# Pieces of 384 tokens in the first third of a projection sweep

## The chip, the cores and the metric

The kernel runs on one core of a Trainium2 chip. The metric is the device time of one execution in microseconds (us). Profiles are of single executions, so their times stand a little off the median of the timed runs.

The engines are called as in the profile: PE is the matrix engine (PEld its weight loads, which overlap the products), DVE the vector engine, ACT the scalar engine, POOL GpSimd; SP only issues DMAs. An instruction queue runs in order.

## The reference

One step of a decoder layer for a prompt of 2048 tokens and a sample group of 8 x 4 = 32 tokens, with shared weights:

```
h   = RMSNorm(x) @ w_in        # D_MODEL 1024 -> 9472 columns
qa, ka, va, za, ub, zb, qc, zc, gt = split(h)
oa  = dilated sliding-window attention(qa, ka, va)   # 12 heads x 64, three (window, dilation) patterns
ob  = silu(LayerNorm(causal depthwise conv, width 31, of GLU(ub)))
oc  = cross-attention(qc) into 256 memory tokens      # 4 heads x 128
mix = gate0 * ((oa * silu(za)) @ w_pa) + gate1 * ((ob * silu(zb)) @ w_pb)
    + gate2 * ((oc * silu(zc)) @ w_pc)                # gates = sigmoid(gt)
y   = x + RMSNorm(mix @ w_out)
```

The sample group attends to caches of past keys and values. All data are float32.

## The kernel before

**Arithmetic.** A float32 product is made of three products of rounded operands: the activations x and the weights w are each split into a high and a low part, and `gemm` adds whi·xh (L166), whi·xl (L167) and wlo·xh (L168). The weights (128 x 128) are the stationary operand and the tokens the moving one, so a product has as many columns as the piece has tokens. With 8 blocks of 128 rows in D_MODEL, a piece of tokens of one block of 128 output columns takes 24 products into one PSUM tile.

**Stages.** `phase_a1` normalizes and transposes x, and computes the q, k, v, u and qc columns (PSUM tile `g`). Behind it come, in the order of the program text: `memory` (which holds the convolution branch's norm `conv_norm` on the tiles `c`, `sm`, `sq`, the memory's keys and values, and both cross-attentions), `sample_attention`, `attention` over 12 heads, then `sweep`, then `phase_c` (gates, projections and the output).

**The sweep.** `sweep` computes the remaining columns of `w_in`: 40 blocks, namely 6 of za, 6 of zb, 4 of zc and 24 of gt. SBUF holds the split activations of one third of the tokens only (tiles `x0h`, `x0l`, 16 in all). So the sweep runs through all 40 blocks for the first third, then refills the 16 tiles from DRAM (`d_x`, issued on POOL's queue at L1083), runs through all 40 blocks again for the second third, and so on. A block's weights are loaded (`wraw`, from ACT's queue) and split on POOL (L55 `whi`, L56 `wlo`) once per third, into two buffers. Within a third the inner loop runs over pieces:

```
SCHUNKS = [(256 * i, 256) for i in range(7)] + [(1792, 288)]     # (first token, tokens)
THIRDS = [(0, 768), (768, 768), (1536, 544)]
...
for s, m in SCHUNKS:
    if a <= s < a + n:
        self.chunk(kind, j, s, m, w, stg, ps, "gg", q=nc.scalar)
        yield
```

**A piece.** `chunk` takes one of two PSUM tiles `gg` (pool `pgg`), each of 512 columns, and one of two SBUF tiles `st` of 384 columns. The 24 products fill `gg`. A gt piece is then read out by one tanh on ACT (L243); a za, zb or zc piece by a tanh on ACT (L245) and a multiply on DVE (L246) that reads `gg` too. A store to DRAM (`d_g`, `d_za`, `d_zb`, `d_zc`) is issued on ACT's queue (L248).

**What sets the order.** The kernel is written with a framework that lays out each engine's order when the program is built. A position in the program text is a priority, and the framework's own estimates of durations say when an operand is ready. The sweep's text stands behind all of `attention`, so it has the lowest priority of the four and fills places in which the others have nothing ready. On the chip that order is fixed: an engine runs its queue in order and waits on semaphores.

Of the kernel before, what the change touches and what calls it, by code (L numbers as in the profile page):

```python
# [28 lines left out]

GROUPS = [(0, 3), (3, 6), (6, 9), (9, 12), (12, 14), (14, 17)]  # L30
CHUNKS = [(0, 384), (384, 384), (768, 384), (1152, 384), (1536, 256), (1792, 288)]
SCHUNKS = [(256 * i, 256) for i in range(7)] + [(1792, 288)]
THIRDS = [(0, 768), (768, 768), (1536, 544)]

CQ, CK, CV, CZA, CUB, CZB, CQC, CZC, CGT = 0, 768, 1536, 2304, 3072, 4608, 5376, 5888, 6400
# [2 lines left out]
class K:  # L38
# [1036 lines left out]
    def sweep(self, blocks, xp, wp, stg, ps):  # L1075
        nc = self.nc
        for th, (a, n) in enumerate(THIRDS):
# [8 lines left out]
            for kind, j in blocks:  # L1086
                w = self.early.pop((kind, j), None) if th == 0 else None
                w = w or self.load_w(wp, self.win(self.BASE[kind] + 128 * j), 8, q=nc.scalar, bufs=2, rp=stg)
                for s, m in SCHUNKS:
                    if a <= s < a + n:  # L1090
# [217 lines left out]
```

## Time and profile before

| | us |
|---|---|
| median of 3 runs | 3149.05 (3148.02 to 3153.83) |
| the profiled execution | 3154.4 |
| its span, from the first to the last instruction | 3152.6 |
| first product of the sweep starts | 868.7 |
| last product of the sweep starts | 2549.7 |
| refills of `x0` are issued | from 1432.1 and up to 2110.5 |

The mean clock that PE was granted is 0.979 of full speed. To read the views: "A <- B" in a list of waits says that A sat idle until B had finished. The chain that ended last is followed back from the last instruction, at each step to what released it or to the instruction before it on its engine; an engine's share of it says how much of the time that engine set. A product's busy time holds its latency and overlaps with its neighbours', so the pace of PE is read from the distance of starts.

### The profile page before, as it was taken

What the parts mean: (1) busy time and instruction counts of PE and PEld (TensorE: products, weight loads), DVE (VectorE), ACT (ScalarE), POOL (GpSimd) and SP (SyncE); (2) the same over time, 40 slices, a digit from 0 to 9 for tenths busy, and PEclk for the clock granted to TensorE, in tenths of its full rate; (3) what the DMA queues carried; (4) which work ended last, traced back from release to release, by engine and by line L of the source; (5) the groups of instructions that cost most, each with busy time, mean ns of one, the idle gap of its engine ahead of it and who ended that gap; (6) DMA issues with size and microseconds to landing.
All of it is one profiled execution on the core that took longest, in us unless ns stands there. A gap on an engine that the chain in (4) does not pass through costs nothing.

```text
span 3152.6 us, 55374 instructions
## 1 busy us (share of the span) xinstructions
PE 3000.2 (95%) x20705; PEld 2839.9 (90%) x20705; DVE 2014.8 (64%) x3734; ACT 1124.2 (36%) x2835; POOL 1350.4 (43%) x1048
## 2 busy tenths in 40 slices
PE   7999999999987999999999999989899979999998
PEld 6899999999987999998999999989898967787897
DVE  5297797796677926465546766666656457556563
ACT  5010010010132433243437575656565523222221
POOL 0121221142356537444256565667676433233240
PEclk9899999999999999999999999999999989999999
DMA  7232222211265454477454656576555487657561
GB/s 250 85 103 80 80 60 61 63 62 50 81 182 167 135 153 144 147 219 239 151 139 116 161 123 163 128 185 150 156 143 152 109 279 227 223 168 227 161 197 53
DMA packets 532218, 454.66 MB, mean 144 GB/s; under 512 B 118191, under 2 KB 458581, under 8 KB 531137
## 3 DMA queue, kind: packets, MB, share of 16 engines
q1 hardware_dynamic: 357502, 335.36, 36.2%
q10 hardware_dynamic: 169840, 105.02, 11.7%
q0 software_dynamic: 4608, 10.75, 1.2%
q8 instruction: 164, 2.69, 0.4%
q14 instruction: 104, 0.85, 0.1%
HBM read 332.96 MB, written 118.04 MB: 143 GB/s over the span
## 4 chain that ended last, share of the span: by engine, by line
PE 70%; DMA 12%; DVE 7%; issue 4%; POOL 3%; ACT 2%; SPq 1%; ACTq 0%; DVEq 0%; POOLq 0%
PE g L166 8%; PE g L167 8%; PE g L168 8%; PE gg L166 6%; PE gg L168 6%; PE gg L167 6%; PE pg L168 3%; PE pg L166 3%; PE pg L167 3%; PE pt L571 2%; DMA cb<-d_cf 2%; PE y L1180 2%; PE y L1179 2%; PE y L1178 2%; PE o L598 1%
## 5 line engine op out<-in xcount | busy, mean ns | idle before, releaser
L166 PE MATMUL gg<-x0h,whi 128*128 128x256 f32 (+1 forms) x2560 | 747.9, 292 | 25.9 <-DVE st L246 12.2
L168 PE MATMUL gg<-x0h,wlo 128*128 128x256 f32 (+1 forms) x2560 | 741.8, 290 | 0.1
L167 PE MATMUL gg<-x0l,whi 128*128 128x256 f32 (+1 forms) x2560 | 741.1, 290 | 0.0
L55 POOL TENSOR_SCALAR whi<-wraw 128x1024 fp32r<-128x1024 f32 x162 | 242.7, 1500 | 928.5 <-PE g L167 524.1
L166 PEld LDWEIGHTS gg<-x0h,whi 128*128 128x128 f32 x2560 | 493.2, 193 | 35.0 <-DVE st L246 13.7
L167 PEld LDWEIGHTS gg<-x0l,whi 128*128 128x128 f32 x2560 | 493.5, 193 | 2.2 <-issue 0.5
L168 PEld LDWEIGHTS gg<-x0h,wlo 128*128 128x128 f32 x2560 | 493.2, 193 | 2.2 <-POOL wlo L56 0.3
L322 DVE SCALAR_TENSOR_TENSOR acc<-G,cw,acc 128x1536 f32<-128x1536 f32 (+15 forms) x354 | 480.8, 1408 | 0.3
L56 POOL TENSOR_TENSOR wlo<-wraw,whi 128x1024 fp32r<-128x1024 f32 x162 | 417.0, 2575 | 9.4 <-PE gg L168 0.2
L155 POOL TENSOR_TENSOR clo<-craw,chi 128x768 fp32r<-128x768 f32 (+1 forms) x96 | 174.1, 1815 | 346.0 <-ACT chi L154 329.8
L627 ACT ACTIVATE P<-T,stm 128x128 f32<-128x128 f32 (+1 forms) x576 | 260.8, 455 | 141.0 <-DVE stm L625 94.8
L239 ACT ACTIVATE st<-g 128x384 f32<-128x384 f32 (+1 forms) x132 | 60.2, 461 | 570.7 <-PE g L168 550.7
L166 PE MATMUL pg<-ac,chi 128*128 128x512 f32 (+1 forms) x640 | 229.4, 359 | 16.6 <-ACT chi L154 8.7
L625 DVE CUSTOM_DVE_ANT_0 T<-s,bias 128x128 f32<-128x128 f32 (+1 forms) x576 | 191.5, 357 | 80.8 <-PE s L617 47.0
L167 PE MATMUL pg<-ac,chi 128*128 128x512 f32 (+1 forms) x640 | 228.8, 358 | 6.3 <-DVE ac L1198 6.3
L168 PE MATMUL pg<-ac,clo 128*128 128x512 f32 (+1 forms) x640 | 227.6, 357 | 3.6 <-POOL clo L155 3.6
L576 DVE TENSOR_TENSOR pl<-pt,ph 128x512 fp32r<-128x512 f32 x240 | 155.6, 652 | 52.4 <-ACT ph L575 48.9
L168 PE MATMUL g<-x0h,wlo 128*128 128x384 f32 x544 | 184.3, 339 | 2.9 <-POOL wlo L56 2.9
L166 PE MATMUL g<-x0h,whi 128*128 128x384 f32 x544 | 183.6, 338 | 2.6 <-ACT st L239 2.3
L167 PE MATMUL g<-x1l,whi 128*128 128x384 f32 x544 | 186.0, 342 | 0.0
L167 PE MATMUL g<-x0l,whi 128*128 128x384 f32 x544 | 185.8, 342 | 0.0
L168 PE MATMUL g<-x1h,wlo 128*128 128x384 f32 x544 | 185.8, 342 | 0.0
(330 smaller groups left out, 7425.0 us busy)
## 6 DMA issues: line engine op xcount, KB each, us to landing
wraw<-in_w_in ACTq DMA_DIRECT2D x119, 512.0 KB
d_g<-st ACTq DMA_DIRECT2D x168, 128.0 KB
cb<-d_cf SPq DMA_DIRECT2D x72, 256.0 KB
g<-d_g SPq DMA_DIRECT2D x72, 256.0 KB
wraw<-in_w_in SPq DMA_DIRECT2D x35, 512.0 KB
kvc<-in_cache_k_win SPq DMA_DIRECT2D x8, 1536.0 KB
kvc<-in_cache_v_win SPq DMA_DIRECT2D x8, 1536.0 KB
raw<-d_q SPq DMA_DIRECT2D x48, 256.0 KB
```

Source lines behind the costliest of these rows:

```text
L55: nc.gpsimd.tensor_scalar(hi, raw, 1.0, 1.0, op0=ALU.mult, op1=ALU.mult)
L56: nc.gpsimd.tensor_sub(lo, raw, hi.bitcast(F32))
L155: nc.gpsimd.tensor_sub(lo, raw, hi.bitcast(F32))
L166: nc.tensor.matmul(ps, hi[:, k, :], h, start=k == 0, stop=False)
L167: nc.tensor.matmul(ps, hi[:, k, :], l, start=False, stop=False)
L168: nc.tensor.matmul(ps, lo[:, k, :], h, start=False, stop=k == kb - 1)
L322: nc.vector.scalar_tensor_tensor(a3[:, lo:hi], G[:, src:src + hi - lo, 2 - m:130 - m], w, a3[:, lo:hi], op0=ALU.mult, op1=ALU.add)
L571: nc.tensor.transpose(t[:, 128 * x:128 * x + 128], pc, self.ident)
L576: nc.vector.tensor_tensor(pl[:, :w], t[:, :w], ph[:, :w].bitcast(F32), op=ALU.subtract)
L625: nc.vector.tensor_tensor_reduce(sc[:, :w], t[:, o:o + w], bias[:, 256 - w:256], 1.0, 3.0e38, ALU.add, ALU.min, m)
L627: nc.scalar.activation(P[:, o:o + w], sc[:, :w], AF.Exp, bias=m, scale=-1.0, accum_out=self.stl[:, col:col + 1])
L1178: nc.tensor.matmul(y[:m, c, :], ah[:, ts_], bh[:, cs], start=k == 0, stop=False)
```

## The change

The pieces of the first third become two of 384 tokens in place of three of 256. The second third keeps three pieces of 256, the last third its pieces of 256 and 288.

```diff
 CHUNKS = [(0, 384), (384, 384), (768, 384), (1152, 384), (1536, 256), (1792, 288)]
-SCHUNKS = [(256 * i, 256) for i in range(7)] + [(1792, 288)]
+SCHUNKS = [(0, 384), (384, 384)] + [(256 * i, 256) for i in range(3, 7)] + [(1792, 288)]
 THIRDS = [(0, 768), (768, 768), (1536, 544)]
```

No tile changes its size: `gg` has 512 columns and `st` has 384 in both.

## The prediction

> **What bounds the kernel now.** The page comes first: which engine fills the span, and which ends it.
>
> ```profile
> span 3152.6 us, 55374 instructions
> PE 3000.2 (95%) x20705; PEld 2839.9 (90%) x20705; DVE 2014.8 (64%) x3734; ACT 1124.2 (36%) x2835; POOL 1350.4 (43%) x1048
> PE 70%; DMA 12%; DVE 7%; issue 4%; POOL 3%; ACT 2%; SPq 1%; ACTq 0%; DVEq 0%; POOLq 0%
> ```
>
> PE is busy for 95% of the span and makes 70% of the chain that ended last; no other engine comes near. A faster PE therefore pays, but only where PE is what the chain follows. So the second view is the table by stretch, for the time in which the sweep's first third runs: the first row ends where DVE has finished its last piece of that third, the second about where the third ends. Of each stretch I show all work, then the tile `gg` (the sweep's products) alone. Columns: length, then busy time and count on PE, on PEld and on the others.
>
> ```profile
> 868.70:1118.00 249.30, 212.54 (x1638) 204.79 (x1637) 202.72 (x264) 91.54 (x171) 141.68 (x126) 0.95 0.53 162
> 1118.00:1435.00 317.00, 314.23 (x2502) 301.96 (x2502) 151.34 (x329) 114.27 (x286) 162.76 (x182) 1.00 0.54 168
> 868.70:1118.00 249.30, 163.89 (x1171) 152.15 (x1172) 19.36 (x48) 18.30 (x48) 0.95 0.53 162
> 1118.00:1435.00 317.00, 227.28 (x1700) 212.50 (x1700) 0.00 (x0) 27.20 (x71) 1.00 0.54 168
> ```
>
> The two stretches differ. In the first PE has 37 us idle and DVE is busy for 203 of 249; in the second PE is never idle for longer than 3 us in all. 1171 of the first third's 2880 products lie in the first stretch, 1700 in the second. The third view, the chain cut to those stretches and to what follows up to the end of the attention, says which engine sets the pace.
>
> ```profile
> by line: issue 16.1%; DVE c L685 9.7%; PE gg L166 6.2%; PE gg L167 5.8%; PE gg L168 5.7%; POOL c L681 4.7%; DVE sm L665 4.6%; DVE sm L673 3.7%; DMA wraw<-in_w_mem_kv 3.5%; ACT sq L684 2.9%; DMA c<-d_c 2.8%; DVE st L246 1.9%; ACT sq L671 1.8
> by line: PE gg L166 19.2%; PE gg L168 19.2%; PE gg L167 19.2%; PE co L990 4.5%; PE tr L791 4.4%; PE sco L1034 4.4%; PE S L804 3.8%; DMA kvc<-in_cache_k_win 3.6%; PE tr L862 2.9%; PE pt L981 2.8%; PE sco L1058 2.5%; PE str L1029 1.9%; PE kv
> by line: PE gg L166 10.5%; PE gg L168 10.2%; PE gg L167 10.1%; PE pt L571 6.4%; DMA cb<-d_cf 4.6%; PE o L598 4.4%; PE s L616 4.2%; PE s L617 4.2%; PE o L597 4.0%; issue 4.0%; DMA rv<-out_v_win_p 2.3%; DMA wraw<-in_w_in 2.1%; DMA x0h<-d_x 2.
> ```
>
> In the first stretch the chain is the convolution branch's norm (`c`, `sm`, `sq` on DVE, ACT and POOL), and `gg` has 17.7% of it. In the second `gg` alone has 57.6% and almost everything else is PE too. Behind it (third row) the chain is again mostly PE, with the attention's products: what the first third gives up earlier, the attention takes over earlier.
>
> **The change part by part.** *Fewer products.* A block of the first third takes 3 pieces of 24 products of 256 columns now, and 2 pieces of 24 of 384 then: 72 become 48, over 40 blocks 2880 become 1920, for the same columns. What that saves hangs on the part of a product's cost that doesn't grow with its columns. The busy times overlap and can't say; the distance of starts can. Each pair below is the first and the last of an unbroken run: 256 columns in the sweep (14 rows), then 384 on the same tile (11 rows) and on another (19 rows), and 256 in a slow moment of the sweep (11 rows), whose granted clock, 0.50, stands in the last row.
>
> ```profile
> 1203.13 0.28 PE L168 MATMUL gg<-x0h,wlo 128*128 128x256 f32 x1
> 1204.69 0.28 PE L166 MATMUL gg<-x0h,whi 128*128 128x256 f32 x1
> ...
> 299.83 0.33 PE L168 MATMUL g<-x0h,wlo 128*128 128x384 f32 x1
> 301.56 0.34 PE L166 MATMUL g<-x0h,whi 128*128 128x384 f32 x1
> ...
> 599.73 0.34 PE L166 MATMUL g<-x1h,whi 128*128 128x384 f32 x1
> 602.90 0.34 PE L166 MATMUL g<-x1h,whi 128*128 128x384 f32 x1
> ...
> 959.45 0.41 PE L167 MATMUL gg<-x0l,whi 128*128 128x256 f32 x1
> 961.58 0.41 PE L168 MATMUL gg<-x0h,wlo 128*128 128x256 f32 x1
> ```
>
> ```profile
> 959.00:961.60 2.60, 2.60 (x14) 2.51 (x13) 2.60 (x5) 2.03 (x3) 0.98 (x1) 0.50 0.96 314
> ```
>
> 1.56/13 is 120 ns for 256 columns; 1.73/10 is 173 ns and 3.17/18 is 176 ns for 384. Three old products cost 360 ns; two new ones 346 or 352. I take 348, nearest the row on the same tile: 12 ns saved per three, or 3.3%. There are 960 such threes, so PE gives up 11.5 us (bounds 7.7 and 13.4).
>
> The Trainium skill, "TensorE: Matmul & The Clock Gate", section "Back-to-back issue gap", speaks against this: at full clock a lone product's gap is its columns by 2.4 GHz and about 2.5 ns, so 109 and 162.5 ns here. By it the saving is some 2.5 ns per three, an estimate of 2.4 us in all. The trace disagrees: 120 and 173.
>
> What of the 11.5 us lies on the path? In the second stretch PE is the path: 1700/3 threes at 12 ns are 6.8 us, and by the chain 57.6% of 317 us at 3.3% is 6.0; I take **6.5**. In the first stretch only the chain's 17.7% of 249.3 us, 44 us, shrinks by 3.3%: **1.5**. The other 3 us of the first stretch become PE idle time in front of the norm's products.
>
> *Fewer, longer evictions.* `gg` has two PSUM buffers, so a piece starts when the piece before last has been read out. That is the one place in which PE waits for the sweep itself (waits of PE in 868 to 1120 us, then the longest of 1120 to 1445):
>
> ```profile
> PE sco L675 <- DVE sm L673: 14.9, 5, 9.0
> PE gg L166 <- DVE st L246: 10.1, 9, 1.8
> ...
> PE S L804 <- ACT KTh L794: 2.8, 1, 2.8
> ```
>
> ```profile
> L243 ACT ACTIVATE st<-gg 128x256 f32<-128x256 f32 x168 | 63.6, 378 | 116.3 <-PE gg L168 109.5 <-DMA d_g<-st 6.4
> L239 ACT ACTIVATE st<-g 128x384 f32<-128x384 f32 x88 | 43.0, 492 | 461.8 <-PE g L168 441.9 <-DMA d_q<-st 19.8
> ...
> L246 DVE SCALAR_TENSOR_TENSOR st<-st,gg 128x256 f32<-128x256 f32 x112 | 45.9, 412 | 43.8 <-ACT st L245 43.4
> ...
> L298 DVE SCALAR_TENSOR_TENSOR G<-gate,g 128x384 f32<-128x384 f32 x24 | 13.3, 555 | 116.2 <-PE g L168 116.2
> ```
>
> One piece covers 24 x 120 = 2.88 us now and 24 x 174 = 4.18 us then, 1.30 more. Against it the eviction grows on ACT by 492-378 = 114 ns (nearest row of 384 columns) and on DVE by 555-412 = 143 ns: net 1.04 us more cover, and the nine waits average 1.1 us. Nearly all of the 10.1 us could go; but the chain is the norm's there, and DVE's `st` has 1.9% of it, 4.7 us. I take **3** (bounds 0 and 10.1). ACT loses 40 x (3 x 378 - 2 x 492) = 6 us of work beside the path.
>
> *Stores.* 120 stores of 128 KB become 80 of 192 KB on ACT's queue. Behind an issue there stand ACT's next evictions and the norm's and softmax's activations; 40 fewer issues are priced at nothing. `st` has two buffers, and the 6.4 us that ACT waited for `d_g` stores above are beside the path while PE has a piece in hand. With longer pieces that wait has more cover.
>
> *Weights.* A block's split on POOL is unchanged:
>
> ```profile
> L56 POOL TENSOR_TENSOR wlo<-wraw,whi 128x1024 fp32r<-128x1024 f32 x48 | 116.6, 2433 | 2.2
> L55 POOL TENSOR_SCALAR whi<-wraw 128x1024 fp32r<-128x1024 f32 x48 | 56.0, 1171 | 157.5 <-PE gg L167 109.1 <-DMA wraw<-in_w_in 33.8 <-PE kv L167 12.4
> ```
>
> It takes 3.6 us against 48 x 174 = 8.35 us of products per block (8.64 now), and POOL mostly waits for PE, not PE for POOL. The cover stays.
>
> *The order.* The program's order is laid out at build time with the sweep as filler, so other piece lengths can re-lay everything behind. The trace doesn't show that price. Its bounds are what PE now waits for in the first stretch, about the 14.9 us of `sco`, in either direction; I take zero, as the second stretch has hardly a wait to gain or to repeat.
>
> **Sum**: 1.5 + 6.5 + 3 = 11.0 us off the profiled 3154.4 (span 3152.6 and 1.8 around it): 3143.4. That execution was 5.35 us above the median of 3149.05; on the median's scale 11 us less is **3138 us**, 0.35% faster. About 0.2%, 6.3 us, is what a measurement of this kernel can tell from no change.
>
> **Rivals.** *All of it counts* (0.12, faster): the nine waits were what made the norm late, and both terms arrive whole: 11.5 + 10.1 = 21.6, 3127. For it: DVE is 81% busy in that stretch, so any stall passes on. Against it: `issue` and `c` lead its chain.
>
> *The chain takes it back* (0.20, same): the first stretch gives nothing, and in the second PE reaches the sample attention's cache loads sooner (`kvc` has 3.6% of that chain, 11.4 us) and waits out half of the 6.5: 3 us less, 3146. For it: the first stretch's chain row. Against it: the second stretch's 314 of 317 us.
>
> *Cost goes by columns* (0.05, same): nothing in a product is fixed, and only the 3 us of evictions come: 3146. For it: the fourth pair, 2.13/10 = 213 ns for 256 at a granted clock of 0.50, less than twice the 120 of full clock, so that a part of the cost is hidden there. Against it: 384 columns at 173 ns. By the rule of the Trainium skill named above the products give 2.4 us, which with the 3 of the evictions ends in this case too.
>
> *The reload is laid bare* (0.18, slower). Between two thirds all 16 `x0` tiles are refilled through POOL's queue:
>
> ```profile
> 1435.50 8.30 DMA x0l<-d_x
> 1445.37 13.94 DMA x0h<-d_x
> ...
> 1326.38 11.35 DMA kvc<-in_cache_k_win
> ```
>
> ```profile
> 1440.00:1450.00 10.00, 8.67 (x65) 7.42 (x63) 4.19 (x11) 4.24 (x11) 7.72 (x17) 1.00 1.13 397
> 1450.00:1462.00 12.00, 7.40 (x45) 6.42 (x46) 4.28 (x13) 2.70 (x8) 2.33 (x10) 0.93 0.86 254
> 1440.00:1450.00 10.00, 3.87 (x24) 3.09 (x24) 0.00 (x0) 0.00 (x0) 1.00 1.13 397
> 1450.00:1462.00 12.00, 2.94 (x18) 2.31 (x18) 0.78 (x2) 0.74 (x2) 0.93 0.86 254
> ```
>
> In these 22 us PE is busy for 16.1, and `gg` has only 6.8 of them: 9.3 us of the sample attention cover the reload. If the third now ends where that attention itself waits for a cache load, the 9.3 are lost and a load of 11.35 us comes on top, 20.6 against 11.0: 3159. It decides the sign from 11 us of loss on. For it: the DMA share is over 1 there, and the third ends some us earlier than before. Against it: the last piece frees its first tile earlier than now, by 4.18 against 2.88 us.
>
> **Chances and range.** Forecast 0.45, all of it 0.12: faster 0.57. Taken back 0.20, by columns 0.05: same 0.25. Reload: slower 0.18. The range goes from a little below *all of it* to the reload's price, 3123 to 3159.
>
> **What would show it.** In the changed profile: `gg` of 128x384 some 174 ns apart; 1920 products in the first third; PE's wait for DVE's `st` before 1120 us down from 10.1 to below 3; the second stretch some 6 us shorter with PE still without idle time; PE's wait on `x0h` as before. The forecast is wrong if the 384-column products start 180 ns apart, if the first stretch's norm simply takes as long while the second doesn't shorten, or if the attention starts earlier by the 11 us and its end doesn't.

## The result, and the profile after

The changed kernel is slower: its median of 6 runs is 3180.2 us (3162.76 to 3183.12) against 3148.53 (3136.91 to 3162.22) for 6 runs of the kernel before beside it, a ratio of 1.0088 with a 95% interval of 1.006 to 1.0116. A second set (run `e4_after_again`, below) gave 1.0071 (1.005 to 1.0093). The forecast was 3138, and its range ended at 3159.

The profiled execution of the changed kernel took 3162.76, the lowest of its six. So its trace shows 8.4 us of loss in the span, where the medians differ by 32; the second profile of the same kernel, with a span of 3170.0, shows 17.4. I read both. First the page of the changed kernel: span, engines, the chain that ended last.

```profile
span 3161.0 us, 53290 instructions
PE 2990.5 (95%) x19745; PEld 2829.5 (90%) x19745; DVE 2005.4 (63%) x3718; ACT 1118.1 (35%) x2795; POOL 1345.9 (43%) x1048
PE 72%; DMA 11%; DVE 7%; issue 4%; POOL 3%; ACT 2%; SPq 1%; ACTq 0%; DVEq 0%; POOLq 0%
```

PE runs 960 products fewer, as counted beforehand, and has the same 95%; its share of the chain rose from 70 to 72%. The totals say nothing of the loss. The table by stretch does, cut at the same five events in both kernels: the last `sco` of the convolution branch's norm (L675), the last product of the cross-attentions (`co`, L990), the first scores of the attention (`s`, L616), its last product (`o`, L598), and a point just behind the first product of the output (`y`, at 2664.3 and 2676.3). Before, then after; the columns are length, then busy time and count on PE, PEld, DVE, ACT and POOL, then PE's granted clock, the DMA share and GB/s.

```profile
868.70:1127.40 258.70, 221.94 (x1717) 214.19 (x1716) 205.66 (x266) 95.60 (x177) 149.38 (x134) 0.95 0.53 162
1127.40:1311.40 184.00, 184.00 (x1474) 177.87 (x1473) 73.61 (x178) 62.17 (x170) 93.10 (x81) 1.00 0.43 133
1311.40:1626.80 315.40, 303.77 (x2301) 284.53 (x2300) 168.28 (x333) 118.53 (x251) 138.88 (x186) 0.99 0.64 194
1626.80:2509.00 882.20, 844.51 (x6896) 834.15 (x6894) 575.45 (x1726) 555.58 (x1712) 565.86 (x461) 0.98 0.58 143
2509.00:2664.50 155.50, 135.09 (x688) 112.87 (x687) 92.79 (x104) 47.53 (x73) 67.49 (x38) 0.95 0.82 256
2664.50:3152.60 488.10, 471.23 (x2352) 394.31 (x2351) 270.96 (x417) 121.94 (x195) 129.28 (x70) 0.98 0.55 172
```

```profile
868.70:1118.00 249.30, 218.22 (x1304) 209.13 (x1304) 202.28 (x250) 90.37 (x159) 149.29 (x134) 0.95 0.53 166
1118.00:1334.50 216.50, 216.50 (x1352) 209.30 (x1351) 72.69 (x181) 66.12 (x166) 107.21 (x89) 1.00 0.42 133
1334.50:1651.60 317.10, 301.14 (x2168) 280.85 (x2167) 165.58 (x347) 118.97 (x247) 137.95 (x191) 0.99 0.66 196
1651.60:2539.00 887.40, 844.61 (x6880) 835.82 (x6879) 573.58 (x1712) 554.42 (x1711) 565.43 (x458) 0.97 0.56 141
2539.00:2677.00 138.00, 101.58 (x423) 79.95 (x422) 96.25 (x105) 43.88 (x62) 51.45 (x29) 0.86 0.85 265
2677.00:3161.00 484.00, 467.21 (x2350) 391.13 (x2348) 268.70 (x417) 121.34 (x194) 128.13 (x70) 0.99 0.55 173
```

Row by row the change is -9.4, **+32.5**, +1.7, +5.2, **-17.5**, -4.1 us: together the 8.4. The second stretch is filled by PE to the last us in both kernels, at full clock, and yet it is 32.5 us longer: PE has more work there. In the fifth PE has 33.5 us less work, and the time shrinks by only 17.5, at a granted clock of 0.86. The same two rows of the second profile differ from before by +32.0 and -14.3.

What the extra work is, the sweep's products (`gg`) alone show, in the second stretch; before, then after:

```profile
1127.40:1311.40 184.00, 131.09 (x977) 122.61 (x975) 0.00 (x0) 15.71 (x41) 1.00 0.43 133
```

```profile
1118.00:1334.50 216.50, 157.97 (x848) 145.12 (x847) 0.00 (x0) 17.55 (x36) 1.00 0.42 133
```

977 products of 256 columns at 120 ns are 117 us; 848 of 384 at 175 ns are 148: 31 us more sweep stand ahead of the cross-attentions' end. To follow it through the kernel I count the sweep in tokens' worth, the sum of the columns of all `gg` products so far divided by 960 (24 products in each of 40 blocks); 2080 is all of it, and one token's worth is about 0.45 us of PE.

| event, us (tokens' worth done) | before | after |
|---|---|---|
| the norm's last `sco` | 1127.4 (332) | 1118.4 (333) |
| cross-attentions' last `co` | 1311.4 (592) | 1334.4 (670) |
| the attention's first `s` | 1626.8 (1018) | 1651.6 (1093) |
| the attention's last `o` | 2508.9 (1994) | 2538.5 (2070) |
| the sweep's last product | 2549.7 (2080) | 2543.1 (2080) |
| from the last `o` to the end | 643.7 | 622.5 |

The sweep itself ends 6.6 us earlier. But 78 tokens' worth of it moved from behind the attention to a place ahead of the cross-attentions' end, and what waits for these moves with it: the cross-attentions end 23 us later, the attention starts 25 and ends 30 us later. Behind the attention 76 tokens' worth are missing, some 34 us of PE, and only 21 us of time.

Why not 34? PE's waits from 2500 to 2700 us, before and after:

```profile
PE pg L167 <- DVE ac L1198: 6.3, 1, 6.3
PE pg L166 <- ACT chi L154: 5.0, 3, 3.1
PE pg L166 <- DVE mix L1150: 3.4, 1, 3.4
```

```profile
PE pg L166 <- DVE mix L1150: 25.1, 1, 25.1
PE pg L166 <- ACT chi L154: 9.2, 2, 8.2
```

Phase C's first products `pg` now wait 25.1 us for DVE's `mix` (26.8 in the second profile). DVE's own order shows what holds `mix` up (timeline of DVE, first the two rows before, then after; start, duration, and in brackets its idle time and what ended it):

```profile
2571.23 0.69 DVE L1139 SCALAR_TENSOR_TENSOR araw<-araw,z 128x512 f32<-128x512 f32 x1 [5.46 <-DMA araw<-d_actb]
2571.96 1.88 DVE L1150 SCALAR_TENSOR_TENSOR mix<-g,pg 128x512 f32<-128x512 f32 x3
```

```profile
2547.46 0.28 DVE L429 TENSOR_TENSOR mn<-stc 32x128 f32<-32x128 f32 x1 [7.34 <-DMA stc<-d_st]
...
2564.90 1.23 DVE L451 TENSOR_TENSOR O<-O,cb 128x1024 f32<-128x1024 f32 x1 [2.35 <-DMA cb<-d_cf]
...
2588.10 1.21 DVE L453 TENSOR_TENSOR O<-O 128x1024 f32<-128x1024 f32 x1
...
2591.94 1.88 DVE L1150 SCALAR_TENSOR_TENSOR mix<-g,pg 128x512 f32<-128x512 f32 x3
```

`mix` stands in DVE's queue behind the attention's last work, which merges the results of the heads (L429 to L453) and waits for loads of `stc` and `cb`, and behind phase C's own gating (`araw` and `ac`, L1139 and L1198), which waits for loads too. It starts 53.4 us behind the attention's last product now (55.7 in the second profile) and started 63.1 us behind it before. Before, 41 us of sweep ran beside that; now 4.6 do.

### The profile page after: what moved, and what is told of

It is laid out like the page before. It is cut to its first block, busy times and chain, and to the rows that moved or that the text cites. A ratio compares the mean times of both kernels' runs of the same rounds, so it can differ in the third digit from the quotient of the medians.

```text
span 3161.0 us, 53290 instructions
## 1 busy us (share of the span) xinstructions
PE 2990.5 (95%) x19745; PEld 2829.5 (90%) x19745; DVE 2005.4 (63%) x3718; ACT 1118.1 (35%) x2795; POOL 1345.9 (43%) x1048
## 4 chain that ended last, share of the span: by engine, by line
PE 72%; DMA 11%; DVE 7%; issue 4%; POOL 3%; ACT 2%; SPq 1%; ACTq 0%; DVEq 0%; POOLq 0%
PE g L166 8%; PE g L167 8%; PE g L168 8%; PE gg L166 6%; PE gg L168 6%; PE gg L167 6%; PE pg L168 3%; PE pg L166 3%; PE pg L167 3%; PE pt L571 2%; PE y L1180 2%; PE y L1179 2%; PE y L1178 2%; DMA cb<-d_cf 2%; PE s L616 2%
## 5 line engine op out<-in xcount | busy, mean ns | idle before, releaser
L166 PE MATMUL gg<-x0h,whi 128*128 128x256 f32 (+2 forms) x2240 | 689.3, 308 | 33.4 <-DVE st L246 19.8
L168 PE MATMUL gg<-x0h,wlo 128*128 128x256 f32 (+2 forms) x2240 | 684.5, 306 | 1.0 <-POOL wlo L56 1.0
L167 PE MATMUL gg<-x0l,whi 128*128 128x256 f32 (+2 forms) x2240 | 683.1, 305 | 0.0
L166 PEld LDWEIGHTS gg<-x0h,whi 128*128 128x128 f32 x2240 | 429.6, 192 | 41.1 <-DVE st L246 14.5
L168 PEld LDWEIGHTS gg<-x0h,wlo 128*128 128x128 f32 x2240 | 429.5, 192 | 2.8 <-POOL wlo L56 1.2
L167 PEld LDWEIGHTS gg<-x0l,whi 128*128 128x128 f32 x2240 | 429.7, 192 | 1.6 <-issue 0.5
L166 PE MATMUL g<-x1h,whi 128*128 128x384 f32 x544 | 182.4, 339 | 0.0
```

Source lines behind the costliest of these rows:

```text
L166: nc.tensor.matmul(ps, hi[:, k, :], h, start=k == 0, stop=False)
L167: nc.tensor.matmul(ps, hi[:, k, :], l, start=False, stop=False)
L168: nc.tensor.matmul(ps, lo[:, k, :], h, start=False, stop=k == kb - 1)
```

## The experiments

Two theories about the loss stood against each other at first. **R**: the loss is the order: long pieces put more of the sweep ahead of the cross-attentions' end, and leave the attention's tail uncovered. Against it, that the products or their evictions cost more than they save (**P** in the expectations), or that work on PE is paid in full wherever it stands. Later expectations name their own rivals by letters, in the place where they test them. Ratios are to the kernel before, with 95% intervals.

**One kind of block each.** 16 of the 40 blocks are za, zb and zc, the first in the order; 24 are gt. `e1_only_z` gives the long pieces to the first kind, `e2_only_gt` (the condition reversed) to the second.

```diff
+WCHUNKS = [(0, 384), (384, 384)] + SCHUNKS[3:]
-                for s, m in SCHUNKS:
+                for s, m in (SCHUNKS if kind == "gt" else WCHUNKS):
```

> Pieces of 384 in the first third for the 16 blocks of za, zb and zc alone; the 24 gt blocks keep 256. Theory R (running ahead: the longer gt pieces let the laid-out order put some 77 tokens' worth of the sweep, 34 us of PE, ahead of the end of the cross-attention, so the attention ends 30 us later and its tail of 50 us loses the sweep as cover): norm ends some 9 us earlier as in the changed kernel, sweep done at the last cross-attention product stays near 592 of 2080 tokens, attention starts and ends earlier than before, total 5 to 12 us below before (ratio 0.996 to 0.998). Rival P (pieces of 384 cost by themselves wherever they run, in eviction and product): 16/40 of the change's loss of 28 us, some 11 us above before (ratio 1.004).

> Pieces of 384 in the first third for the 24 gt blocks alone. Theory R: all of the change's loss and none of its gain in the norm, sweep done at the last cross-attention product near 670 of 2080 tokens, attention ends 25 to 40 us later than before, the sweep ends with it, total 25 to 40 us above before (ratio 1.008 to 1.013). Rival P: 24/40 of the loss, some 17 us above before (ratio 1.005).

Measured: `e1_only_z` 1.0016 (0.9999 to 1.0033), `e2_only_gt` 1.0101 (1.0082 to 1.0121). Both lie outside P's figures (1.004 and 1.005). R's figure for the second came true; for the first it had 0.996 to 0.998 and an earlier end of the norm, and neither came (the norm ended at 1129.1). The loss comes with gt, and so does the shift: at the cross-attentions' end `e1_only_z` has 577 tokens' worth done at 1307.3 us, `e2_only_gt` 673 at 1342.4. The sweep in that stretch, first `e1_only_z`, then `e2_only_gt`:

```profile
1129.10:1307.30 178.20, 126.13 (x924) 117.08 (x924) 0.00 (x0) 14.94 (x39) 1.00 0.43 133
```

```profile
1127.50:1342.40 214.90, 158.66 (x846) 145.58 (x845) 0.00 (x0) 17.70 (x36) 1.00 0.40 128
```

The z blocks are through by then in these two, so only a gt piece's length matters there. Against the kernel before, `e2_only_gt` has 30.9 us more in this stretch and 20 us less behind the last `o` (the wait for `mix` is 27.8), with its norm ending at the old time. In `e1_only_z` the order moved a little the other way: 20 tokens' worth, 9 us of PE, went from ahead of the attention's last product to behind it. Its attention ends 6 us earlier (2502.9), and the part behind that is 7.8 us longer (651.5). It saves its share of the products, and no gain is seen.

**The changed kernel again,** for a second profile, and **the last blocks held back** (`e3_hold13`): in the last third the weights of the last 13 gt blocks may load only when head 10 has stored its state, so that sweep is left for the attention's tail.

> The changed kernel once more, for a second profile beside the others on one chip: ratio 1.006 to 1.012 to before. The first profile took 3162.8 us against a median of 3180.2, so it may show a part of the loss that the first doesn't. Theory R: a profile near 3180 us has the same order and the same late end of the attention (some 30 us later than before), and loses the rest in the uncovered tail or at the attention's waits on loads.

Measured: 1.0071, as given above. The order is the same (670 tokens' worth at the cross-attentions' end, 2070 at the attention's), and the attention's last product comes at 2540.9.

```diff
+        if hold is not None:
+            (q or nc.sync).dma_start(raw[0:1, 0, :], hold)
...
+                hold = self.d_st[10][0:1, 0:128] if th == 2 and i >= len(blocks) - HOLD else None
```

> The changed kernel, with the last 13 gt blocks of the last third (177 tokens' worth of the sweep, some 78 us of PE) held back: their weight load stands behind a small read of what attention head 10 writes at its end. The pieces stay 384. Theory R: 117 tokens' worth (some 50 us of PE) run behind the attention's last product and cover its tail, the attention ends 30 to 45 us earlier than in the changed kernel, total at or below before: 0 to 15 us below (ratio 0.995 to 1.000). Rival P: the loss of 28 us stays (ratio 1.009), as no piece has changed. Rival Q (the attention only starts late because the cross-attention itself takes longer, and no order behind it can help): the attention ends as late as in the changed kernel and the held blocks come on top, ratio 1.010 or more.

Measured: 1.0117 (1.0093 to 1.014), no repair, and the ratio that rival Q had named. The attention ended at 2531.1, 7 us earlier than in the changed kernel where R had 30 to 45; its norm had ended 10 us later, so between the first `s` and the last `o` some 20 us were gained for 107 tokens' worth, 48 us of PE, fewer. The tail was covered again (from the last `o` or last `gg` to the first product of the output `y` 113.4 us; 114.6 before, 133.1 after). But the cover was taken from the last heads: this row runs from the attention's first scores to its last product.

```profile
1664.10:2531.10 867.00, 816.38 (x6500) 803.75 (x6498) 569.03 (x1712) 549.23 (x1694) 540.48 (x443) 0.95 0.55 138
```

PE idles for 51 of 867 us at a clock of 0.95, against 43 of 887 at 0.97 in the changed kernel, and the sweep left over made the rest longer: 662.7 us from the last `o` to the end, where the changed kernel has 622.5. Filler taken out of the attention came off its time by less than half, and the filler put behind it cost 40 us.

**The old order back, with the new pieces** (`e5_paced`): from block 20 on, the weights of the first third's blocks wait for successive steps of the cross-attention to have stored their output.

```diff
+                it = int((i - PACE[0]) * PACE[1]) if th == 0 and i >= PACE[0] else 99
+                hold = self.d_act[12 + it // 4][0:1, 512 * (it % 4):512 * (it % 4) + 128] if it < 16 else None
```

> The changed kernel, with the weight load of the first third's blocks from number 20 on standing behind a small read of what a given step of the cross-attention has written, so that the sweep can't run ahead of it: 596 of 2080 tokens' worth of the sweep stand ahead of the last cross-attention product (before 592, changed kernel 670), 1999 ahead of the attention's last (before 1994, changed 2070). Pieces of the first third stay 384. Theory R: attention ends 25 to 35 us earlier than in the changed kernel, near 2505 us; the sweep's last product comes 35 to 45 us behind it; the time from the sweep's last product to the first output product goes from 133 to 136 us back to about 115; ratio 0.997 to 1.001. Rival P (the pieces of 384 cost by themselves): the loss stays, ratio 1.007 to 1.009.

Measured: 1.0058 (1.0036 to 1.008), 3168.44. The order came back (596 tokens' worth at the cross-attentions' end, 592 before), and with it the tail: 642.5 us behind the last `o` (643.7 before), and `pg` waits 3.2 us for `mix` in place of 25. The attention's end came back by only 9 us, though, to 2529.3 of 2538.5. A part of the rest was lost ahead of the gates: the norm ended at 1130.7, 12 us later than in the changed kernel (on this below). Another part lies in the stretch of the gates:

```profile
1130.70:1325.70 195.00, 188.36 (x1162) 177.59 (x1160) 74.22 (x180) 62.02 (x158) 91.10 (x81) 0.99 0.38 123
```

195 us in place of the 184 of the kernel before, 6.6 of them idle on PE, which the stretch never was. The long pieces don't take the 11 us: adding up the distances from each product's start to the next one's in this stretch, the sweep's take 117.6 us (119.5 before), but the cross-attentions' `co` 21.5 in place of 14.0. That the gates leave too little sweep ready while `co` waits is my reading of it. Of the 19 us by which this span is above the one before, the norm's end has 3, this stretch 11, the two behind it 6, and the tail gives 1 back. The ratio lies inside the interval of `e4_after_again`, so this run shows the mechanism by its marks and not by its time; R's figure for the time was missed.

**Another third, another length.** `e6_second_third` leaves the first third at 256 and gives the second 2 x 384; `e7_pieces_192` gives the first 4 x 192.

```diff
+SCHUNKS = [(256 * i, 256) for i in range(3)] + [(768, 384), (1152, 384)] + [(1536, 256), (1792, 288)]
...
+SCHUNKS = [(192 * i, 192) for i in range(4)] + [(256 * i, 256) for i in range(3, 7)] + [(1792, 288)]
```

> Pieces of 256 in the first third as before; the second third, which runs beside the attention, in two of 384. In the laid-out order the sweep is as before up to the end of the cross-attention (592 tokens' worth) and wholly used up ahead of the attention's last product (2080 of 2080). Theory R: the loss is in the same place as in the changed kernel, the uncovered tail: the time from the last product of sweep and attention to the first output product grows from 115 to about 135 us, while the 960 products less give 8 to 11 us; ratio 1.003 to 1.010. Rival S (what hurts is the longer piece beside the norm and the cross-attention, in the first third alone): no loss, ratio 0.996 to 0.998.

> The other direction: four pieces of 192 in the first third. In the laid-out order 444 tokens' worth of the sweep stand ahead of the cross-attention's end and 1781 ahead of the attention's last product, so 299 are left behind it. Theory R: the attention ends 70 to 95 us earlier than before (213 tokens at 0.44 us), its tail is covered in full, the time from the sweep's last product to the first output product is 110 to 116 us; products cost a little more (four of about 93 ns for three of 120, some 11 us), so ratio 1.000 to 1.006. Rival V (what stands ahead of the attention costs it nothing, it ends where its own chain ends): the attention ends within 15 us of before and 299 tokens at 0.44 us come on top of it less the 41 us of before, 90 us, ratio 1.03.

`e6_second_third`: 1.0119 (1.0098 to 1.014). The cross-attentions end as before (1311.0, 592 tokens' worth). Now the attention takes up the extra sweep: its first `s` comes at 1637.3, its last `o` at 2565.6, 928.3 us in place of 882.0. It holds 46 tokens' worth more, some 21 us; where the rest of the 46 us goes isn't shown, but the sweep ends at 2506.4, and in the 59 us left up to the last `o` PE idles for 7, where it had no idle time in the last 59 before. Behind the last `o` there are 625.1 us with a wait of 23.8 for `mix`. This is a loss of the same kind in another place, larger than R's 1.003 to 1.010 in its middle value; rival S, no loss, is out.

`e7_pieces_192`: 1.0339 (1.0313 to 1.0364). Here the expectation was wrong by its price: I had put a product of 192 columns at 93 ns, and it takes 112 (17 starts in a row; first and last).

```profile
1202.73 0.27 PE L168 MATMUL gg<-x0h,wlo 128*128 128x192 f32 x1
...
1204.52 0.27 PE L166 MATMUL gg<-x0h,whi 128*128 128x192 f32 x1
```

(1.79 us over 16 steps.) So the first third costs 3840 x 112 ns in place of 2880 x 120, 84 us more, and the run can't weigh the order by its time. Rival V's marks came: the attention ended within 15 us of before (2518.7), and behind it stand 734.7 us, 91 more. But 214 tokens' worth fewer ahead of that, some 96 us, and 84 us of dearer products leave only 12 us of difference there, so the run leans to V and doesn't decide. What it does show is the count, the sweep between the norm's end and the cross-attentions' end:

```profile
1127.40:1309.30 181.90, 125.92 (x997) 119.96 (x996) 4.96 (x14) 13.84 (x42) 0.99 0.38 116
```

997 products of 192 columns, 977 of 256, 846 to 848 of 384. The order laid out at build time takes a number of products ahead of that mark that falls far less than their length grows, so the tokens' worth done there aren't fixed: 444, 592 and 670. On the chip these products are 112, 117 and 148 us. That a 384-column product counts for only 977/848 = 1.15 of a 256-column one in the layout, and 175/120 = 1.46 on the chip, is my reading of the counts; the layout's own estimates weren't looked at.

**Is sweep behind the attention worth its time?** `e8_bare_tail` is the kernel before with 31 us of products taken out of the last gt pieces, those that run beside the attention's tail.

```diff
-        self.gemm(p[:, :n], w, [self.x_at(k, s, n) for k in range(8)])
+        self.gemm(p[:, :n], w, [self.x_at(k, s, n) for k in range(1 if kind == "gt" and j >= 18 and s >= 1536 else 8)])
```

> The kernel before, pieces of 256, with a part of the sweep left out: in the last third the last 6 gt blocks do 1 of their 8 steps over D_MODEL (3 products for 24), eviction and store unchanged; 71 tokens' worth, some 31 us of PE. In the laid-out order everything up to the attention's last product is as before, and 15 tokens' worth instead of 86 stand behind it. Theory R (the sweep behind the attention covers its tail, and phase C's first evictions wait on DVE behind that tail): attention's last product at 2509 as before, PE waits some 20 to 27 us for DVE's first mix of phase C, the time from the sweep's last product to the first output product grows from 115 to 132 to 138 us, so that only 8 to 14 of the 31 us are saved: ratio 0.995 to 0.998. Rival U (phase C starts late in the changed kernel for another reason, and the cover is worth nothing): the whole 31 us are saved, ratio 0.990.

Measured: 0.9996 (0.998 to 1.0011), 3143.76 against 3148.29. Of 31 us at most some 6 (the interval's lower end) came off the time; R had allowed 0.995 to 0.998. But the mark that R had named, 20 to 27 us of waiting for `mix`, didn't come either. From 2500 to 2700 us PE doesn't wait for `mix` at all, and its longest waits show something else:

```profile
PE pg L166 <- ACT ac L1197: 12.0, 3, 7.6
PE gg L166 <- POOL whi L55: 8.1, 2, 5.0
...
PE gg L168 <- POOL wlo L56: 4.6, 4, 1.5
```

The thinned blocks keep their weights, and with three products in a piece PE now waits 12.7 us for POOL's splits of them, where it waited for none before. So the sweep's last product still came 28.2 us behind the last `o` (40.9 before), and `pg` then waited for `ac`. The run shows that these products can go and hardly any time goes with them. It doesn't show that the cover as such is worth nothing, and it can't rule out rival U, as the blocks that were left met a limit of their own.

**Is PE's work ahead of the attention worth its time?** `e12_thin_gt`, again the kernel before, leaves out the last of 8 steps in the first third's gt pieces: 24 x 3 x 3 products, with lengths and pieces as they were. These are 216 products in all, 25.9 us at 120 ns each; the expectation has 216 of each of three kinds, and 26.6 us.

```diff
+        self.gemm(p[:, :n], w, [self.x_at(k, s, n) for k in range(7 if kind == "gt" and s < 768 else 8)])
```

> The kernel before, pieces of 256, with PE work left out and no piece made longer: gt pieces of the first third do 7 of their 8 steps over D_MODEL, 1728/8 = 216 products of each of the three kinds less, some 26.6 us of PE in all, more than the 15 us that the 384 products save. In the laid-out order the cross-attention's end has as many sweep products ahead of it as before (593 tokens' worth by count of columns, before 592), the attention's last product 1964 (before 1994), 58 are left behind it (before 86). Theory W (the step of the prediction: PE is the path from the second stretch on, so PE work that goes is time that goes): attention's last product 13 us earlier (30 tokens at 0.44 us), the part behind it 8 to 12 us shorter, total 21 to 25 us less, ratio 0.992 to 0.994. Theory X (the other work of each stretch is close behind PE, so that PE work that goes comes back as waits and as half-clock time, and what is left out behind the attention only uncovers its tail): less than 9 us of the 26.6 saved, ratio 0.997 to 1.000.

Measured: 0.9984 (0.9968 to 1.0), 3141.64 against 3148.38: 7 us, 0 to 10 by the interval, of 25.9. Theory W (0.992 to 0.994) is out, and X's range was met. The stretch that PE fills did not shorten (first row; 184.0 before), since the order put 971 products into it again, and the attention's last product came at 2508.5 (2508.9 before), though 30 tokens' worth fewer stood ahead of it. Between the cross-attentions and the first `s` PE idled for 19 us in place of 12, at a granted clock of 0.96 in place of 0.99.

```profile
1131.00:1314.30 183.30, 183.30 (x1468) 177.21 (x1467) 72.82 (x178) 65.37 (x177) 99.40 (x86) 1.00 0.45 143
...
2508.50:3144.40 635.90, 597.52 (x2945) 494.63 (x2943) 371.81 (x521) 168.07 (x263) 191.67 (x104) 0.97 0.60 191
```

**The norm's end.** It came 9 us earlier in the changed kernel (1118.4, and 1118.6 in its second profile) than in the kernel before and in the other versions so far (1126.7 to 1131.0). The third of nine passes of one DVE instruction (L685; L686 in `e1_only_z`, whose listing is a line longer) explains most of it. The DVE timelines of before, after and `e1_only_z`:

```profile
976.94 7.79 DVE L685 SCALAR_TENSOR_TENSOR c<-sq,c 128x1536 f32<-128x1536 f32 x1 [0.70 <-ACT sq L684]
```

```profile
975.18 1.75 DVE L685 SCALAR_TENSOR_TENSOR c<-sq,c 128x1536 f32<-128x1536 f32 x1
```

```profile
975.75 12.21 DVE L686 SCALAR_TENSOR_TENSOR c<-sq,c 128x1536 f32<-128x1536 f32 x1
```

It takes 1.75 us alone and, in this pass, up to 12.2 beside POOL's splits of weights. In `e3_hold13`, which has the changed kernel's pieces and differs from it in the last third only, the same pass took 12.2 us and the norm ended at 1128.4: the 9 us aren't owed to the pieces. Three runs moved the high half of the memory's weights to ACT (`act=True`), to end that meeting: in `e5_paced` (`e9_paced_kv`), in `e1_only_z` (`e10_only_z_kv`) and in the kernel before (`e11_before_kv`).

```diff
-            w = self.load_w(wp, I["w_mem_kv"][0, :, 128 * c:128 * c + 128], 8)
+            w = self.load_w(wp, I["w_mem_kv"][0, :, 128 * c:128 * c + 128], 8, act=True)
```

> The paced kernel of before, and the memory's weights get their high half from ACT instead of POOL, so that POOL splits less beside the norm. In the paced kernel the norm's third pass at L685 on DVE took 12.2 us, in the changed kernel 1.75, in the kernel before 7.8, while POOL ran weight splits beside it. Theory C (this collision, not the pieces, is what the paced kernel lost against the changed one in the first stretch): L685 there under 5 us, the norm ends 6 to 12 us earlier than in the paced kernel (1131), ratio to before 0.999 to 1.004 after 1.0058. Rival: L685 is stretched all the same or PE's products set the norm's end, ratio unchanged at 1.004 to 1.008.

> Pieces of 384 for za, zb and zc in the first third, with the memory's weights split as in the run beside it. Theory C: the norm's third pass at L685 falls from 12.2 to under 5 us, the norm ends 6 to 12 us earlier than in the run with za, zb and zc alone (1129), ratio to before 0.996 to 1.000 after 1.0016. Rival: nothing changes, 1.000 to 1.003.

> The kernel before, pieces of 256 everywhere, with the memory's weights split as in the two runs beside it: what that edit is worth by itself. Theory C: the third pass at L685 falls from 7.8 to under 5 us, the norm ends 3 to 6 us earlier, ratio 0.997 to 1.000. Against the run with za, zb and zc this tells what the 384 products themselves are worth once the collision is away: 6 us less PE work, of which the stretch that the norm sets may show nothing.

Measured: 1.008 (1.006 to 1.01), 1.004 (1.0022 to 1.0057) and 1.0034 (1.0017 to 1.0052), all above theory C's ranges. In the first two, three passes (the second to the fourth) then took 9.4 to 10.3 us: the meeting was moved and not ended, and both intervals overlap those without the edit. In the third C's marks came true: the pass took 2.2 us in place of 7.8 and the norm ended at 1122.6, 4.8 us earlier. Yet its attention ended 7 us later than before (2515.9, with 2009 tokens' worth done) and the kernel is slower: an earlier end of the norm was no gain there. No version here that computes the whole layer beats the kernel before.

## Why the prediction was wrong, step by step

- **Fewer products** (11.5 us): right in kind, somewhat less in size. 384 columns are 175 ns apart:

```profile
1202.82 0.34 PE L166 MATMUL gg<-x0h,whi 128*128 128x384 f32 x1
...
1205.45 0.33 PE L166 MATMUL gg<-x0h,whi 128*128 128x384 f32 x1
```

  2.63 us over 15 steps, so 9 to 10 ns per three in place of 12, some 9 us in all, within the bounds given. The sweep's last product comes 6.6 us earlier.
- **"In the second stretch PE is the path"** (6.5): this step failed. PE was indeed busy without a gap, but it took for granted that the same tokens stand in the stretch. What stands there is set by the order, and it fills what is saved with more filler: `e12_thin_gt` took out 25.9 us of products, and the stretch kept its length. `e1_only_z` lost behind the attention what it gained ahead of it.
- **The order, priced at zero, with bounds of 14.9 either way:** this is the step that turned the sign. The re-laid order put 78 tokens' worth more ahead of the cross-attentions' end, which cost 32.5 us there, of which the part behind the attention gave back 21. The bounds came from PE's waits in the first stretch; the price is no wait but work in another place, and has nothing to do with them. `e2_only_gt` shows the same (30.9 us more there, 20 back), `e6_second_third` a like loss inside the attention. No run that put the order back got the time back, so this rests on the counts and the rows by stretch.
- **Evictions** (3): failed. PE's waits for DVE's `st` before 1120 us, after:

```profile
PE gg L166 <- DVE st L246: 10.1, 6, 5.6
```

  Six waits in place of nine, and the same 10.1 us. From 1118 to 2500 us this wait rose from 2.1 to 9.7.
- **First stretch** (1.5): 9.4 us came, most of it from the DVE instruction above and not from products, which is luck: `e3_hold13`, with the same pieces, ended its norm at 1128.4.
- **Weights, stores, reload** (nothing): a small sign of a cost in the weights, as PE's one wait for a split (`whi`) before 1120 us grew from 3.9 to 6.8 us; none in the others. PE's wait on `x0h` from 1118 to 2500 us is 6.9 us in both kernels, so the one slower rival, the reload laid bare, was the wrong reason for a slower kernel.
- **"What the first third gives up earlier, the attention takes over earlier":** the attention began 25 us later. Of the signs named, the count and the spacing of the products came true, the shorter second stretch and the smaller wait for `st` didn't.

Open: the profiled executions show 8.4 and 17.4 us of loss in the span, the medians 32 and 22; I can't say what the slower executions of the changed kernel add. One candidate is the norm's third pass, 1.75 us in both profiles of this kernel and 12.2 in `e3_hold13`; no profile of a slower execution shows it. And no run has the new pieces in the old order without gates, so the saving's worth there was seen only by way of `e1_only_z`, `e5_paced` and `e12_thin_gt`.

## What to carry to other kernels

Where work is laid out as filler, ask of a change in its pieces first how much of it will stand ahead of each mark that something waits for, and what covers the stretch that it leaves; a busy PE is no proof that a us saved in the filler is a us saved at the end. Before pricing filler at its duration, take some of it out and see what the end does. Don't price an order that a planner makes at zero when lengths change: bound it, as an estimate, by the whole of the filler that could move (here 86 tokens' worth behind the attention, 39 us), not by the waits of today.

## What the runs showed of the hardware

The norm's DVE instruction, which has two SBUF inputs, and a run of POOL's splits kept each other out. In `e1_only_z` POOL worked without a gap from 974.16 us, and the instruction above, begun at 975.75, ended at 987.96, 1.6 us after POOL's last one (the timeline of POOL; the first two and the last of the run):

```profile
974.16 2.08 POOL L56 TENSOR_SCALAR whi<-wraw 128x1024 fp32r<-128x1024 f32 x2
976.19 0.42 POOL L56 TENSOR_SCALAR vh<-mrow 128x256 fp32r<-128x256 f32 x1
...
985.31 1.04 POOL L56 TENSOR_SCALAR whi<-wraw 128x1024 fp32r<-128x1024 f32 x1
```

In the kernel before it ended at 984.73, again 1.6 us after POOL's last one (983.13). In the changed kernel it started at 975.18, ahead of POOL's small split, and that was the one to wait, 1.85 us in place of 0.42:

```profile
975.35 1.85 POOL L55 TENSOR_SCALAR vh<-mrow 128x256 fp32r<-128x256 f32 x1
```

The Trainium skill, "SBUF — State Buffer", section "SBUF: two separate sides", says that DVE and GpSimd hold a shared pair of ports exclusively, for a DVE instruction with two SBUF inputs too, and that whoever starts first blocks the other for its whole instruction. These rows agree, and add that a run of POOL instructions kept DVE out for all of its length.

From 256 to 192 columns a product gets hardly cheaper: 112 ns at 192, 120 at 256, 175 at 384. The Trainium skill, "TensorE: Matmul & The Clock Gate", section "LDWEIGHTS (loading the stationary operand)", puts a weight load at its columns by 1.2 GHz, so 107 ns for 128 as an estimate. The 112 ns are near that, and each product here has a load of its own; that the load is what sets the pace of 192 columns no run shows.
